# One inverse loop with other tiles beside it, a later down projection, and eight early ring tiles in a two-block kernel

## The chip, the cores and the metric

The kernel runs on one core of one Trainium2 chip. The metric is the device time of one execution in microseconds, the median of the runs shown. TensorE (PE), VectorE (DVE), ScalarE (ACT), GpSimd (POOL) and SyncE (SP) each work through a queue of their own in a fixed order. Transfers that SP or ACT issue run on 16 DMA engines.

## The reference, cut to what matters

Two blocks run one after the other on 512 tokens of width 1024. The first (RWKV, an MLP, an attention layer, another MLP) is the same before and after. The second is a mixer of two branches, and then 16 experts:

```python
proj = h @ w_in                      # qkv of DeltaNet, z, b, a, c_q, c_kv, k_r, gates
# DeltaNet, 8 heads of 128, forwards and backwards in time; per chunk:
lower = where(strict, (k_beta @ k.T) * decay, 0)
t_inv = inverse(eye + lower)         # unit triangular
u, w  = t_inv @ v_beta, t_inv @ (k_beta * exp(gc))
intra = where(tril, (q @ k.T) * decay, 0)
v_new = u - w @ state;  o = qd @ state + intra @ v_new   # then the state moves on
y_dn  = (rms_norm(o_fwd + o_bwd) * silu(z)) @ w_o_dn
y_mla = softmax_attention(c_q, c_kv, k_r) @ w_o_mla
x = x + gt1 * ((sigmoid(g_dn) * y_dn + sigmoid(g_mla) * y_mla) @ w_out)
# experts: each takes the 64 tokens that it scores highest
gate, idx = top_k(softmax(h @ w_router).T, 64)
hid = silu(xe @ w_gate) * (xe @ w_up)
out[idx] += (hid @ w_down) * gate
```

## The kernel before

A scheduler orders each engine's queue when the kernel is built, by a priority (the place in the program, plus an offset inside `behind`) and by its own idea of how long each instruction takes. On the chip the order is fixed: an instruction that has to wait holds up all that is behind it on its engine.

**The mixer** (`mixer`, from about 1620 us). `dn_group` runs the DeltaNet twice, for heads 0 to 3 and 4 to 7. Beside it, at lower priority, `mla_gen` feeds TensorE with dense tiles (`dense_gen`, the matmuls at L1323): 128 output columns each, 24 matmuls, and weights that SP loads, ACT rounds (L181) and POOL splits (L183). The order of the dense tiles is the list `cks`: 12 convolution tiles of the second group (`use_b`; `dn_conv` takes five DVE instructions for each), 8 z tiles (`use_z`, one ACT and one DVE instruction), 8 gate tiles (`use_g`, one ACT instruction), 7 latent tiles (`use_c`), 8 more gate tiles, then the projections of the MLA branch and its attention. The results go to DRAM through `keep`, a transfer that ACT issues (L1261), and come back through `fetch`, which SP issues.

One group goes through: the scaled keys and queries; four heads, each with its decay matrices E for both directions (L1545 to L1551, a strict mask on POOL) and the triangular matrices UB and masked products IN (L1556 to L1566; POOL adds the diagonal to E, L1564); the inverse `tri_inverse2`; and a scan over four chunks. UB holds 32 triangular matrices of 128x128, 16 upper ones (forwards) and 16 lower ones (backwards). The inverse first inverts the 32x32 blocks on the diagonals, one matrix to a partition: a DVE transpose into P (L1395), one loop of 31 steps that solves the one kind (L1400, L1402), a second loop of 31 steps for the other kind (L1407, L1409; on the other half each loop does nothing), and eight transposes back (L1413 into T1, L1414 into UB). Then products of 32-wide blocks (L1422, L1429) and of 64-wide ones (L1449, L1457, L1465) build the rest.

After both groups w_o_dn, w_o_mla and w_out follow (8 tiles each).

**The experts** (`experts`, from about 2498 us). They run in eight pairs. Weight tiles of 1 MiB (256 rows of one matrix of one expert) pass through a ring of RR = 16 slots of 8 KiB per partition; SP issues a slot's next load when TensorE has read it (L2081). A pair takes four steps of gate, four of up and four of down, each step two tiles and 16 matmul instructions (L2134, L2162), 24 tiles a pair, 192 in all. Between up and down stand: the one-hot matrix for the scatter and the gates (`slots`, L2095 to L2102), silu and product (L2146, L2147), and transposes (L2150, copied at L2152). RE = 5 of the slots lie where nothing is needed any more while w_out runs; SP issues their loads between the last w_out weight loads (`between`). The other 11 lie under the weight buffers, so that their first loads wait for the end of w_out. Gathers of the later pairs (`pieces`, L2068, L2069) are mixed into the steps of the first three pairs.

Of the kernel before, what the change touches and what calls it, by code (L numbers as in the profile page):

```python
# [34 lines left out]
RR = 16  # L35
RE = 5
RO = 1
SL = 38
# [84 lines left out]
class K:  # L123
# [1212 lines left out]
    def dn_gates(self, pt):  # L1336
# [46 lines left out]
        return dict(B=B, G=Gm, EG=EG, ET=ET, nEG=nEG, nB=nB, BL=BL)  # L1383

    def tri_inverse2(self, bp, UB):
# [30 lines left out]
        W1 = bp.tile([128, 32, 32], F32, name=self.nm("W1"), tag="p4", bufs=2)  # L1416

        xy = [(b + (d == 1), b + (d == 0), 16 * d) for b in (0, 2) for d in range(2)]
        pt = self.ps()
        for u in range(16):  # L1420
            for x, y, o in xy:
                nc.tensor.matmul(pt[Q[y], u * 32:u * 32 + 32], UB[Q[x], o + u, Q[y]], T1[Q[x], o + u],  # L1422
                                 start=(u == 0), stop=(u == 15), skip_group_check=True)
        nc.scalar.activation(W1[:, 0:16], pt.rearrange("p (u j) -> p u j", j=32), AF.Copy)
        yield 0.7
        pt = self.ps()
        for u in range(16):
            for x, y, o in xy:
                nc.tensor.matmul(pt[Q[x], u * 32:u * 32 + 32], W1[Q[y], u], UB[Q[y], o + u, Q[y]],  # L1429
                                 start=(u == 0), stop=(u == 15), skip_group_check=True)  # L1430
        for x, y, o in xy:
            p3 = pt[Q[x]].rearrange("p (u j) -> p u j", j=32)
            if x % 2:
# [5 lines left out]
        H = [slice(0, 64), slice(64, 128)]  # L1439
        xy = [(H[d], H[1 - d], 16 * d) for d in range(2)]  # L1440
        T2 = bp.tile([128, 16, 64], F32, name=self.nm("T2"), tag="p4", bufs=2)
        W2 = bp.tile([128, 16, 64], F32, name=self.nm("W2"), tag="p4", bufs=2)
        idn = self.cst("ident")
        pair = lambda pt: pt.rearrange("p (u j) -> p u j", j=64)
        for ub in (0, 8):
            pt = self.ps()
            for u in range(8):
                for x, y, o in xy:
                    nc.tensor.matmul(pt[x, u * 64:u * 64 + 64], UB[x, o + ub + u, x], idn[x, x],  # L1449
                                     start=(u == 0), stop=(u == 7), skip_group_check=True)  # L1450
            nc.scalar.activation(T2[:, ub:ub + 8], pair(pt), AF.Copy)
        yield 0.7
        for ub in (0, 8):
            pt = self.ps()
            for u in range(8):
                for x, y, o in xy:
                    nc.tensor.matmul(pt[y, u * 64:u * 64 + 64], UB[x, o + ub + u, y], T2[x, ub + u],  # L1457
                                     start=(u == 0), stop=(u == 7), skip_group_check=True)
            nc.vector.tensor_copy(W2[:, ub:ub + 8], pair(pt))
        yield 0.7  # L1460
        for ub in (0, 8):
            pt = self.ps()
            for u in range(8):
                for x, y, o in xy:
                    nc.tensor.matmul(pt[x, u * 64:u * 64 + 64], W2[y, ub + u], UB[y, o + ub + u, y],  # L1465
                                     start=(u == 0), stop=(u == 7), skip_group_check=True)
            for i, (x, y, o) in enumerate(xy):
                if i:
                    nc.vector.tensor_copy(UB[x, o + ub:o + ub + 8, y], pair(pt[x]))
                else:  # L1470
                    nc.scalar.activation(UB[x, o + ub:o + ub + 8, y], pair(pt[x]), AF.Copy)
# [19 lines left out]
    def dn_group(self, bp, tiles, gi, gs, Zs, out):  # L1491
# [41 lines left out]
        for i in range(4):  # L1533
# [900 lines left out]
```

## Time and profile before

| | |
|---|---|
| median of 3 runs | 2994.79 us (2993.59 to 2998.83) |
| the profiled execution | 2999.24 us, its span 2997.4 us |
| TensorE busy | 2766.3 us, 92% of the span |
| VectorE, ScalarE, GpSimd busy | 1615.5, 1049.1, 726.7 us |
| read from HBM | 471.26 MB |

Busy times say which engine a stage leans on; a stage's bound is read from what ends the idle time of its busiest engine. A DMA share near 1 means that all 16 DMA engines copy all the time. A wait is put down to what came last by the profile.

### The profile page before, as it was taken

What the parts mean: (1) busy time and instruction counts of PE and PEld (TensorE: products, weight loads), DVE (VectorE), ACT (ScalarE), POOL (GpSimd) and SP (SyncE); (2) the same over time, 40 slices, a digit from 0 to 9 for tenths busy, and PEclk for the clock granted to TensorE, in tenths of its full rate; (3) what the DMA queues carried; (4) which work ended last, traced back from release to release, by engine and by line L of the source; (5) the groups of instructions that cost most, each with busy time, mean ns of one, the idle gap of its engine ahead of it and who ended that gap; (6) DMA issues with size and microseconds to landing.
All of it is one profiled execution on the core that took longest, in us unless ns stands there. A gap on an engine that the chain in (4) does not pass through costs nothing. (4 is left out here: it accounts for less than half of the span.)

```text
span 2997.4 us, 38061 instructions
## 1 busy us (share of the span) xinstructions
PE 2766.3 (92%) x15046; PEld 1971.0 (66%) x15046; DVE 1615.5 (54%) x2449; ACT 1049.1 (35%) x1703; POOL 726.7 (24%) x563
## 2 busy tenths in 40 slices
PE   6998888999999999999999997998799997999997
PEld 1765666788876777788886775766677874444333
DVE  4568745465673367566636789638755442111112
ACT  2555523422234466422223542353344322110001
POOL 2456633211110043111113353144141121000000
PEclk9998777999999999999999999999999998999999
DMA  6324215355672321465432223142252359999998
GB/s 214 120 85 151 77 58 176 99 175 190 196 242 66 101 61 50 133 205 182 156 97 84 80 81 113 51 134 74 61 179 85 106 192 355 350 389 409 409 409 304
DMA packets 361010, 502.05 MB, mean 167 GB/s; under 512 B 24768, under 2 KB 236992, under 8 KB 360832
## 3 DMA queue, kind: packets, MB, share of 16 engines
q1 hardware_dynamic: 349600, 479.01, 47.0%
q10 hardware_dynamic: 11232, 20.62, 1.9%
q8 instruction: 118, 1.93, 0.3%
q14 instruction: 60, 0.49, 0.0%
HBM read 471.26 MB, written 26.21 MB: 166 GB/s over the span
## 5 line engine op out<-in xcount | busy, mean ns | idle before, releaser
L244 PE MATMUL psb<-s,wh 128*128 128x512 f32 x1384 | 542.8, 392 | 2.7 <-DVE s L988 1.9
L245 PE MATMUL psb<-s,wl 128*128 128x512 f32 x1384 | 540.4, 390 | 0.0
L246 PE MATMUL psb<-s,wh 128*128 128x512 f32 (+1 forms) x1320 | 514.7, 390 | 1.5 <-POOL s L481 0.6
L181 ACT ACTIVATE wh<-wr 128x1024 fp32r<-128x1024 f32 (+1 forms) x221 | 288.1, 1304 | 397.9 <-PE psb L246 263.9
L183 DVE TENSOR_TENSOR wl<-wr,wh 128x1024 fp32r<-128x1024 f32 (+1 forms) x145 | 260.7, 1799 | 262.8 <-ACT wh L181 260.4
L244 PEld LDWEIGHTS psb<-s,wh 128*128 128x128 f32 x1384 | 259.4, 187 | 70.7 <-issue 11.4
L245 PEld LDWEIGHTS psb<-s,wl 128*128 128x128 f32 x1384 | 259.5, 188 | 56.5 <-issue 2.2
L246 PEld LDWEIGHTS psb<-s,wh 128*128 128x128 f32 (+1 forms) x1320 | 247.4, 187 | 58.5 <-issue 2.9
L183 POOL TENSOR_TENSOR wl<-wr,wh 128x1024 fp32r<-128x1024 f32 (+1 forms) x76 | 185.5, 2443 | 401.4 <-ACT wh L181 386.1
L2134 PE MATMUL psb<-rg,s 128*64 128x512 f32 x1024 | 242.9, 597 | 5.7 <-DMA rg<-in_w_up_dram 4.4
L1323 PE MATMUL psf<-f,wh 128*128 128x512 f32 (+1 forms) x688 | 232.3, 412 | 10.7 <-ACT wh L181 10.7
L1019 POOL TENSOR_TENSOR s<-s 128x512 f32<-128x512 f32 x64 | 102.2, 1596 | 514.8 <-ACT s L1017 434.1
L2134 PEld LDWEIGHTS psb<-rg,s 128*64 128x64 f32 x1024 | 83.1, 136 | 142.6 <-issue 120.4
L1323 PEld LDWEIGHTS psf<-f,wh 128*128 128x128 f32 (+1 forms) x688 | 133.3, 195 | 42.5 <-ACT wh L181 11.6
L1323 PE MATMUL psf<-f,wl 128*128 128x512 f32 (+1 forms) x344 | 142.7, 415 | 16.6 <-POOL wl L183 16.5
L2162 PE MATMUL psb<-rg,s 128*64 128x512 f32 (+1 forms) x544 | 129.5, 620 | 0.0
L378 DVE SCALAR_TENSOR_TENSOR mt<-mr,crep,mt 128x512 f32<-128x512 f32 x168 | 126.4, 753 | 3.6
L201 ACT ACTIVATE s<-s 128x512 fp32r<-128x512 f32 x112 | 69.8, 625 | 136.2 <-POOL s L1019 73.1
L1026 DVE SCALAR_TENSOR_TENSOR s<-psb,aff,s 128x512 f32<-128x512 f32 x64 | 45.9, 751 | 129.1 <-PE psb L246 129.1
L1323 PE MATMUL psb<-f,wh 128*128 128x512 f32 (+1 forms) x336 | 106.5, 397 | 7.8 <-DVE f L479 5.9
L1017 ACT ACTIVATE s<-psb 128x512 f32<-128x512 f32 x64 | 37.6, 588 | 164.0 <-PE psb L246 164.0
L2162 PEld LDWEIGHTS psb<-rg,s 128*64 128x64 f32 x544 | 46.2, 147 | 73.9 <-issue 69.8
(565 smaller groups left out, 4926.4 us busy)
## 6 DMA issues: line engine op xcount, KB each, us to landing
rg<-in_w_gate_dram SPq DMA_DIRECT2D x64, 1024.0 KB
rg<-in_w_up_dram SPq DMA_DIRECT2D x64, 1024.0 KB
rg<-in_w_down_dram SPq DMA_DIRECT2D x64, 1024.0 KB
mr<-in_mod_w_dram SPq DMA_DIRECT2D x96, 512.0 KB
wr<-in_mlp_down_dram SPq DMA_DIRECT2D x32, 1024.0 KB
wr<-in_mlp_up_dram SPq DMA_DIRECT2D x31, 1024.0 KB
wr<-in_w_in_dram SPq DMA_DIRECT2D x54, 512.0 KB
mr<-in_w_mod_dram SPq DMA_DIRECT2D x40, 512.0 KB
```

Of the source, the lines that this page charges most:

```text
L181: nc.scalar.activation(hi, raw, AF.Copy)
L183: (lo_eng or self.lo_eng or nc.vector).tensor_tensor(lo, raw, hi.bitcast(F32), op=OP.subtract)
L201: nc.scalar.activation(hi, src, AF.Copy)
L244: nc.tensor.matmul(pt[:mw], hi[k][:, j:j + mw], a, start=(k == 0), stop=False)
L245: nc.tensor.matmul(pt[:mw], lo[k][:, j:j + mw], a, start=False, stop=False)
L246: nc.tensor.matmul(pt[:mw], hi[k][:, j:j + mw], b, start=False, stop=(k == nk - 1))
L378: nc.vector.scalar_tensor_tensor(acc[:, hb], raw[:, d], c, acc[:, hb], op0=OP.mult, op1=OP.add)
L1019: nc.gpsimd.tensor_tensor(sq, r, r, op=OP.mult)
L1026: nc.vector.scalar_tensor_tensor(xT[m], pt, gt[:, m:m + 1], xT[m], op0=OP.mult, op1=OP.add)
L1323: nc.tensor.matmul(pt[:rows, :cols], x, y, start=(k == 0 and q == 0), stop=(k == nk - 1 and q == 2))
L2134: nc.tensor.matmul(B[n][q], XE[hp][k0 // 2][:, o:o + 64], w[e][:, k, n * 512:n * 512 + 512], start=(k0 + k == 0), stop=(k0 + k == 7), skip ...
L2162: last = nc.tensor.matmul(pt[q, :n], HT[(k + i) // 4][:, o:o + 64], w[e][i], start=(k + i == 0), stop=(k + i == 7), skip_group_check=True)
```

## The change

- **Inverse.** The matrices of the backward direction are built transposed, so that all 32 are upper triangular and the second loop goes. Of the eight transposes back, two go (T1 is only needed for the blocks 0 and 2). The masked products IN of the backward direction need E the other way round: four TensorE transposes and an ACT copy for each head. POOL's addition of the diagonal goes (the mask now holds it). In the scan beta is now a row factor of the backward inverse: one DVE multiplication over half of UB per group, and one ACT copy in place of four scaled ones in each step of the backward direction. The products of 32-wide and 64-wide blocks change their places: they read two groups of rows instead of four, or one instead of two, and write different columns; per group 16 products that transpose 64-wide blocks, some copies, and a POOL copy and memset are added.
- **Order in a group.** `decays(i + 1)` is issued before `triangles(i)`.
- **Dense tiles beside it.** 8 convolution tiles, 8 gate tiles, the other 4 convolution tiles, 8 z tiles, 7 latent tiles, the other 8 gate tiles.
- **Experts.** The first gate step of the next pair is issued before a pair's transposes and down steps. `slots` multiplies the one-hot matrix by the scores, transposes it, and takes both the scatter matrix and the gates from there on DVE, without the eight small matmul instructions.
- **Ring.** RR 17, RE 8, slots SL 40; the early loads stand behind the 12th to 5th from last weight load (before: the 7th to 3rd from last).

```diff
-RR = 16
-RE = 5
-RO = 1
-SL = 38
+RR = 17
+RE = 8
+SL = 40
...
-        for k in range(31, 0, -1):
-            n, m = k, 32 - k
-            tv = tm[:, :n * m].rearrange("p (j i) -> p j i", i=m)
-            nc.vector.tensor_tensor(tv, P[:, 0:n, k:k + 1].to_broadcast([128, n, m]),
-                                    R[:, k:k + 1, k:32].to_broadcast([128, n, m]), op=OP.mult)
-            nc.vector.tensor_tensor(R[:, 0:n, k:32], R[:, 0:n, k:32], tv, op=OP.add)
-            yield 0.55
...
-        for d in range(4):
-            nc.vector.transpose(T1[Q[d]].rearrange("p u i -> p i u"), R[Q[d]].rearrange("p j i -> p i j"))
+        for d in (0, 2, 1, 3):
+            if d % 2 == 0:
+                nc.vector.transpose(T1[Q[d]].rearrange("p u i -> p i u"), R[Q[d]].rearrange("p j i -> p i j"))
             nc.vector.transpose(UB[Q[d], :, Q[d]].rearrange("p u j -> p j u"), R[Q[d]])
...
-        xy = [(b + (d == 1), b + (d == 0), 16 * d) for b in (0, 2) for d in range(2)]
+        xy = [(b, b + 1, b + 1 - d, 16 * d) for b in (0, 2) for d in range(2)]
...
+                nc.tensor.matmul(pt[y, u * 64:u * 64 + 64], UB[y, 16 + ub + u, y], idn[y, y],
+                                 start=(u == 0), stop=(u == 7), skip_group_check=True)
...
+        nc.gpsimd.tensor_copy(UB[x, 16:32, x], T2[1][x])
+        nc.gpsimd.memset(UB[x, 16:32, y], 0.0)
...
-                nc.gpsimd.tensor_tensor(v3(E), v3(E), bc(self.cst(strict)), op=OP.mult)
+                nc.gpsimd.tensor_tensor(v3(E), v3(E), bc(self.cst("le")), op=OP.mult)
...
+            pe = self.ps()
+            for cs in csl:
+                nc.tensor.transpose(pe[:, cs], Es[i][1][:, cs], idn)
...
-                nc.gpsimd.tensor_tensor(v3(E), v3(E), bc(idn), op=OP.add)
+                if d:
+                    E = self.s()
+                    nc.scalar.activation(E, pe, AF.Copy)
...
+        u1 = UB[:, 16:32].rearrange("p (i c) t -> p i c t", c=4)
+        nc.vector.tensor_tensor(u1, u1, gs["B"][:, :, 8 + 4 * gi:12 + 4 * gi].rearrange("p c i -> p i c").unsqueeze(3)
+                                .to_broadcast([128, 4, 4, 128]), op=OP.mult)
...
-        cks = self.fm_chunks(W, [[(m * 128, 128)] for m in self.dn_cols(1)], hf, use_b)
-        cks += self.fm_chunks(W, tl(3072, 8), hf, use_z)
-        cks += self.fm_chunks(W, tl(4960, 16), hf, use_g)
+        cv = self.fm_chunks(W, [[(m * 128, 128)] for m in self.dn_cols(1)], hf, use_b)
+        gc = self.fm_chunks(W, tl(4960, 16), hf, use_g)
+        cks = cv[:8] + gc[:8] + cv[8:] + self.fm_chunks(W, tl(3072, 8), hf, use_z) + gc[8:]
...
-        between = self.loads[-8:][RO:][:RE]
+        between = self.loads[-12:][:RE]
...
+            nc.vector.tensor_tensor(hv, hv, bc(aff), op=OP.mult)
...
+            nc.vector.tensor_scalar(OT[pr], pt, 0.0, None, op0=OP.is_gt)
+            nc.vector.tensor_reduce(gate[:, pr:pr + 1], pt, axis=AX.X, op=OP.add)
...
+        self.run(products(0))
+        for pr in range(8):
+            more = iter(())
+            if pr < 7:
+                more = products(pr + 1)
+                next(more)
...
                 for n in range(2):
                     add(Yp[n], range(4 * n, 4 * n + 4))
+                self.run(more)
```

`products(pr)` holds what stood in the loop of the pairs before: the steps of gate and up with the gathers between them, `slots`, silu and product. It gives way after each step, so that `next(more)` issues one gate step (two loads, 16 matmul instructions, a gather while there are any) and `self.run(more)` the other seven.

## Rows read from the trace of the kernel before

**Rows 1.** windows: length, then busy time (instructions) of each engine, clock, DMA share, GB/s

```profile
1760.00:1900.00 140.00, 112.57 (x774) 87.97 (x775) 126.95 (x204) 39.16 (x60) 50.59 (x24) 0.93 0.34 99
2040.00:2140.00 100.00, 71.19 (x575) 53.99 (x574) 92.48 (x151) 25.26 (x35) 29.65 (x13) 0.86 0.28 82
1740.00:2260.00 520.00, 446.88 (x3053) 356.24 (x3053) 370.59 (x663) 199.15 (x383) 187.64 (x103) 0.95 0.33 99
```

**Rows 2.** TensorE's waits, 1740 to 2260 us: total us, times, longest us

```profile
PE psb L1422 <- DVE T L1413: 27.2, 6, 13.2
PE psf L1323 <- POOL wl L183: 16.5, 11, 2.1
```

**Rows 3.** groups of instructions by line, 1600 to 2320 us: busy us, mean ns

```profile
L1407 DVE TENSOR_TENSOR tm<-P,R 128x31 f32<-128x31 f32 (+15 forms) x62 | 29.8, 480 | 2.0
L1409 DVE TENSOR_TENSOR R<-R,tm 128x31 f32<-128x31 f32 (+15 forms) x62 | 31.7, 511 | 2.1
L1413 DVE STREAM_TRANSPOSE T<-R 32x1024 f32<-32x1024 f32 x8 | 16.8, 2099 | 0.1
L1485 DVE SCALAR_TENSOR_TENSOR f<-psf,P,f 128x510 f32<-128x510 f32 (+1 forms) x48 | 35.6, 742 | 4.6 <-ACT f L1482 4.2
L1536 PE MATMUL psb<-C,s 128*128 128x128 f32 x32 | 4.9, 274 | 0.4 <-DVE in L1566 0.4
```

**Rows 4.** timelines by engine, one z tile beside the second loop: start us, us, instruction

```profile
1846.67 0.33 ACTq L1261 DMA_DIRECT2D kd<-f  x1
1847.04 0.60 ACT L1685 ACTIVATE f<-psf 128x512 f32<-128x512 f32 x1 [6.61 <-DVE tm L1407]
...
1848.67 2.51 POOL L183 TENSOR_TENSOR wl<-wr,wh 128x1024 fp32r<-128x1024 f32 x1 [5.77 <-ACT wh L181]
...
1849.00 2.44 DVE L1407 TENSOR_TENSOR tm<-P,R 128x231 f32<-128x231 f32 x1
1851.91 0.41 DVE L1407 TENSOR_TENSOR tm<-P,R 128x240 f32<-128x240 f32 x1
...
1851.24 0.50 PE L1323 MATMUL psf<-f,wl 128*128 128x512 f32 x1 [1.61 <-POOL wl L183]
```

**Rows 5.** TensorE's timeline: waits in the two groups, and 64-wide products of the inverse

```profile
1877.43 0.28 PE L1422 MATMUL psb<-T,UB 32*32 32x32 f32 x2 [10.26 <-DVE T L1413]
...
1897.60 2.08 PE L1449 MATMUL psb<-C,UB 64*64 64x64 f32 x60
...
2074.25 0.79 PE L1323 MATMUL psf<-f,wh 128*128 128x512 f32 x1 [10.69 <-ACT wh L181]
```

**Rows 6.** windows ahead of and in the experts' stage, columns as in group 1

```profile
2380.00:2420.00 40.00, 40.00 (x178) 32.88 (x177) 19.21 (x16) 11.28 (x13) 12.96 (x10) 1.00 0.33 99
2490.00:2690.00 200.00, 185.00 (x914) 86.61 (x916) 28.86 (x57) 30.49 (x53) 1.23 (x1) 0.94 0.92 359
2690.00:2960.00 270.00, 255.44 (x1092) 108.14 (x1088) 44.71 (x75) 20.12 (x34) 0.00 (x0) 0.98 1.03 408
```

**Rows 7.** timeline, the turn from up to down: the first pair, then the second

```profile
2532.45 3.65 PE L2134 MATMUL psb<-rg,s 128*64 128x512 f32 x16
...
2540.02 0.66 PE L2150 MATMUL psb<-C,s 128*128 128x128 f32 x4 [2.52 <-DVE s L2147]
2542.57 1.11 PE L2150 MATMUL psb<-C,s 128*128 128x128 f32 x4 [1.90 <-DVE s L2147]
2543.62 6.02 PE L2162 MATMUL psb<-rg,s 128*64 128x512 f32 x16
...
2606.83 0.66 PE L2095 MATMUL psb<-C,s 128*128 128x128 f32 x4
...
2613.10 3.68 PE L2162 MATMUL psb<-rg,s 128*64 128x512 f32 x8
```

**Rows 8.** SP's timeline: loads into the ring

```profile
2470.43 11.77 SPq L2081 DMA_DIRECT2D rg<-in_w_up_dram  x8
2501.42 6.58 SPq L2081 DMA_DIRECT2D rg<-in_w_down_dram  x4
```

More of the change, by code (lines that the diff above doesn't have):

```diff
@@ L1427, in tri_inverse2 @@
         for u in range(16):
[L1428 to L1429 removed]
+            for x, y, z, o in xy:
+                nc.tensor.matmul(pt[Q[z], u * 32:u * 32 + 32], T1[Q[y], o + u], UB[Q[y], o + u, Q[y]],
                                  start=(u == 0), stop=(u == 15), skip_group_check=True)
[L1431 to L1433 removed]
+        for x, y, z, o in xy:
+            p3 = pt[Q[z]].rearrange("p (u j) -> p u j", j=32)
+            if o:
                 nc.scalar.activation(UB[Q[x], o:o + 16, Q[y]], p3, AF.Copy)
@@ L1437, in tri_inverse2 @@
         yield 1.2
[L1439 to L1442, printed above, removed]
+        x, y = slice(0, 64), slice(64, 128)
+        T2 = [bp.tile([128, 16, 64], F32, name=self.nm("T2"), tag="p4", bufs=2) for _ in range(2)]
         idn = self.cst("ident")
@@ L1447, in tri_inverse2 @@
             for u in range(8):
-                for x, y, o in xy:
-                    nc.tensor.matmul(pt[x, u * 64:u * 64 + 64], UB[x, o + ub + u, x], idn[x, x],
+                for d, q in enumerate((x, y)):
+                    nc.tensor.matmul(pt[q, u * 64:u * 64 + 64], UB[x, 16 * d + ub + u, x], idn[x, x],
                                      start=(u == 0), stop=(u == 7), skip_group_check=True)
-            nc.scalar.activation(T2[:, ub:ub + 8], pair(pt), AF.Copy)
+            nc.vector.tensor_copy(T2[0][x, ub:ub + 8], pair(pt[x]))
+            nc.scalar.activation(T2[1][x, ub:ub + 8], pair(pt[y]), AF.Copy)
         yield 0.7
@@ L1455, in tri_inverse2 @@
             for u in range(8):
-                for x, y, o in xy:
-                    nc.tensor.matmul(pt[y, u * 64:u * 64 + 64], UB[x, o + ub + u, y], T2[x, ub + u],
+                for d, q in enumerate((y, x)):
+                    nc.tensor.matmul(pt[q, u * 64:u * 64 + 64], UB[x, 16 * d + ub + u, y], T2[d][x, ub + u],
                                      start=(u == 0), stop=(u == 7), skip_group_check=True)
-            nc.vector.tensor_copy(W2[:, ub:ub + 8], pair(pt))
+            nc.scalar.activation(T2[0][y, ub:ub + 8], pair(pt[y]), AF.Copy)
+            nc.vector.tensor_copy(T2[1][y, ub:ub + 8], pair(pt[x]))
         yield 0.7
+        pts = []
         for ub in (0, 8):
@@ L1463, in tri_inverse2 @@
             for u in range(8):
[L1464 to L1471, printed above, removed]
+                v = T2[0][y, ub + u], UB[y, ub + u, y]
+                nc.tensor.matmul(pt[x, u * 64:u * 64 + 64], *v, start=(u == 0), stop=(u == 7), skip_group_check=True)
+                v = UB[y, 16 + ub + u, y], T2[1][y, ub + u]
+                nc.tensor.matmul(pt[y, u * 64:u * 64 + 64], *v, start=(u == 0), stop=(u == 7), skip_group_check=True)
+            nc.vector.tensor_copy(UB[x, ub:ub + 8, y], pair(pt[x]))
+            nc.scalar.activation(UB[y, 16 + ub:24 + ub, x], pair(pt[y]), AF.Copy)
+            pt = self.ps()
+            for u in range(8):
+                nc.tensor.matmul(pt[y, u * 64:u * 64 + 64], UB[y, 16 + ub + u, y], idn[y, y],
+                                 start=(u == 0), stop=(u == 7), skip_group_check=True)
+            pts.append(pt)
+        for ub, pt in zip((0, 8), pts):
+            nc.scalar.activation(UB[y, 16 + ub:24 + ub, y], pair(pt[y]), AF.Copy)
+        nc.gpsimd.tensor_copy(UB[x, 16:32, x], T2[1][x])
+        nc.gpsimd.memset(UB[x, 16:32, y], 0.0)
         yield 1.0
@@ L1532, in dn_group, with decays @@
         csl = [slice(c * 128, c * 128 + 128) for c in range(4)]
-        for i in range(4):
+        def decays(i):
             pv = self.ps()
@@ L2121, in experts, with products @@
             gather(0, f)
-        for pr in range(8):
+        SG = [None] * 8
+        def products(pr):
             hp = pr // 2
-            G = [self.ps() for _ in range(2)]
-            U = [self.ps() for _ in range(2)]
+            G, U = [], []
             for W, B in ((A["w_gate_2"], G), (A["w_up_2"], U)):
+                B.extend(self.ps() for _ in range(2))
                 for k0 in range(0, 8, 2):
@@ L2147, in experts @@
                 nc.vector.tensor_tensor(sg, U[n], sg, op=OP.mult)
+                SG[pr].append(sg)
+        self.run(products(0))
[4 more added lines that the diff above has]
+                next(more)
+            HT = []
+            for sg in SG[pr]:
                 pt = self.ps()
```

60 lines of the change are left out of this document (34 added, 26 removed).

## The prediction

> **What bounds the kernel now.** I read three views in this order: the windows by stage, then for each stage where TensorE isn't full its waits, then the timelines of the engines named there. The change touches two stretches: the mixer (about 1620 to 2470 us) and the experts (about 2500 us to the end).
>
> In the mixer TensorE carries the time: dense tiles of low priority fill what DeltaNet leaves, and outside the two groups it is full. From 1740 to 2260 us it works 446.9 of 520 us, so 73.1 us are idle [rows 1]. In the two stretches around the inverses (1760 to 1900, 2040 to 2140 us) VectorE is busy 91% and 92% of the time, and TensorE is idle 27.4 and 28.8 us, 56 us together: there VectorE is the bound. The granted clock is 0.93 and 0.86 there, which means that TensorE ran part of these stretches at the lower of its two levels (1.2 GHz instead of 2.4). The waits name the causes: 27.2 us for the transposes L1413 that end the loops, 16.5 us for POOL's split of a dense weight [rows 2], and one of 10.69 us for ACT's rounding of one [rows 5]. The second cause is VectorE again: in the timelines ACT's queue stands at the store of a z tile (issued at 1846.67) until VectorE, deep in the loop, has made the tile; only then do ACT's next steps and POOL's split (1848.67) follow, and TensorE has waited 1.61 us at 1851.24 [rows 4].
>
> In the experts' stage two limits take turns. From 2690 to 2960 us the DMA share is 1.03 at 408 GB/s: the engines copy all the time [rows 6]. A 1 MiB tile takes 1.049 MB / 408 GB/s = 2.57 us. From 2490 to 2690 us the share is only 0.92: the ring is full and TensorE frees it too slowly. Lost copying: (1.03 - 0.92) / 1.03 x 200 = 21 us. As copying sets the end, only these 21 us, and what is copied ahead, can be won.
>
> **Experts: the later down projection.** At a turn TensorE ends the up step at 2532.45 + 3.65 = 2536.1 us, waits 2.52 and 1.90 us for silu and product, and ends the first down step at 2543.62 + 6.02 = 2549.6 us (6.02 instead of 3.65, its clock being low after the gaps) [rows 7]. That is 13.5 us for a step of 3.65, 9.9 us lost. In the second pair the turn runs from 2606.83 to 2613.10, and 8 instructions take 3.68 us instead of 1.83: 6.3 + 1.85 = 8.1 us lost. Afterwards a gate step of the next pair (3.65 us of work that is only moved) covers VectorE's part. This part grows: the scatter matrix and the gate sum come ahead of the products, some four steps of 0.7 us (the 0.742 us of a 512-wide step [rows 3] as the nearest price), 2.8 us, which just fits under 3.65. What remains is three times four transposes (0.66 each) and a copy (0.60), 2.6 us. Saved: 7.3 and 5.5 us; in the third pair the copying has nearly caught up, I take 1. On SP two gate loads go ahead of eight down loads; the ring takes tiles in the order in which they are read, so nothing waits longer for that.
>
> **Experts: the ring.** SP issues the tiles that wait for the end of w_out from 2470.43 us on, and the next only at 2501.42, when TensorE has freed a slot [rows 8]. Between these 16 tiles are in the ring before and 17 after, however many came early: one tile, 2.6 us. The three further early loads thus buy no 3 x 2.57 = 7.7 us but only the room for the 17th slot, since the DMA engines would be idle sooner. Their place on SP is between weight loads that TensorE needs; what is queued behind them is the next w_o_mla or w_out load. From 2380 to 2420 us, where some of them now fall, the share is 0.33 with TensorE full [rows 6], so I cost them at 0 (bounds 0 and 7.7). The Trainium skill, "DMA: Bandwidth & Descriptors", section "Issuing engines are not separate DMA queues", says that all transfers share the same 16 engines and interleave; by that alone the full 7.7 us would be charged and the sum below be 29 in place of 37; the share of 0.33 speaks for the smaller charge.
>
> Experts together: 7.3 + 5.5 + 1 + 2.6 = 16 us won. Bounds: 3 (only the ring) and 21 (all that was lost).
>
> **Mixer: the inverse.** The second loop costs VectorE 29.8 + 31.7 = 61.5 us in both groups, and four of the eight L1413 transposes 8.4 us [rows 3]. This is time of VectorE; what counts is TensorE's wait. (a) The 27.2 us arise because TensorE's queue holds the first L1422 products ahead of dense tiles that could run, and the loops end later than the scheduler thought. With half of the loops I take half: 13.6 us won (bounds 0 and 27.2). What is late next is the first loop, which stays. (b) Gate tiles have no VectorE step, so ACT's queue no longer stands at their store: the three waits beside the z tiles (1.61 us and two alike, 5.3 us) go. Four convolution tiles, each with four VectorE steps of 0.742 us and one more, leave the loop for the scan; I take 4 us of the other waits for POOL. Together 9 us (bounds 0 and 16.5). (c) The 10.69 us stand beside latent tiles, which still meet the second inverse; I take 3 (bounds 0 and 10.7). (d) With half of the long gaps some of the time at the lower clock goes; 3 us (bounds 0 and 10, from 0.07 x 140 = 9.8 us in the first stretch).
>
> Added: 32 transposes of E, at 4.9 us for 32 alike [rows 3]; 32 instructions of 64-wide transposes per group, at 2.08 us for 60 [rows 5], 2.2 us in both. Sum 7 us of TensorE, charged in full. The products of small blocks now read the same rows in pairs. If such pairs ran one after the other, five stages of about 2 us would double, 20 us in both groups; the nearest row says otherwise: half-width experts' products that share rows take 3.65 / 16 = 0.23 us for 512 columns, where a full-width product takes 4.9 / 32 = 0.15 for 128. So 0, bound 20. VectorE's new multiplication (4 x 0.742 = 3.0 us) and POOL's copy (near the 2.5 us of a split [rows 4]) lie between inverse and scan, on DeltaNet's own chain; dense tiles cover them on TensorE. Without that cover they cost 11 us. ACT's eight copies (0.60 each) replace more scaled copies than they are, and POOL loses sixteen additions. The eight gate tiles pass four convolution tiles on SP, ACT, POOL and TensorE, each with load, split, 24 products and store; the fetches of the second group wait for these four. They come right behind the gate tiles, so I expect them done within the scan: 0.
>
> One rule speaks against (b). In the timelines a loop instruction of 0.41 us takes 2.44 while POOL's split runs [rows 4]. The Trainium skill, "SBUF — State Buffer", section "SBUF: two separate sides", has VectorE and GpSimd share a port pair that whoever starts first holds for the whole instruction. Dense tiles that no longer stall bring more splits into a loop, each 2 us; with two or three more per group, half of it felt by TensorE, the mixer would give 16 instead of 21 us.
>
> Mixer together: 13.6 + 9 + 3 + 3 - 7 = 21 us won.
>
> **The sum.** 16 + 21 = 37 us. The profiled execution would go from 2999.2 to 2962 us (its span from 2997.4 to 2960); the median, 4.4 us lower, from 2994.8 to 2958.
>
> **Rivals.**
> 1. TensorE fills nearly all: the waits of 27.2, 16.5 and 10.7 and a few others go (60 us), less 7 added. For it: VectorE's load in the two stretches falls by about a third. Against: the order on TensorE is still made ahead of time. 53 + 21 = 74 won: 2921 us.
> 2. The mixer's waits only move: the L1422 wait and the splits stall elsewhere for as long, and the experts give 16: 2979 us. For it: a VectorE loop is still there, and z and latent tiles now meet the second inverse.
> 3. The turn isn't shortened, since VectorE's longer part comes after the gate step: only the ring's 2.6 us in the experts, 24 in all: 2971 us.
> 4. Slower: the tiles that need VectorE (8 z, 7 latent), shifted back by the gate tiles, meet the second group's loop. Each z tile stalls ACT's queue and with it TensorE by 2 us (17 us); the two normalisations of latent tiles each make a wait like that of 10.69 us with a low clock behind it (30 us instead of the 15 so far); the L1422 waits stay, and 7 us are added, while the 5 us beside the z tiles go: 17 + 15 + 7 - 5 = 34 us, of which the experts give back 16: 3013 us. It decides from the point where new waits in the mixer exceed the gains by 16 us. Against it: VectorE loses 70 us of work in these stretches.
>
> **How the numbers follow.** Forecast 0.50, rival 1 0.20, rival 2 0.13, rival 3 0.10, rival 4 0.07. Predicted: 2958 us; its own range is 2940 to 2972. The range 2918 to 2984 leaves out rival 4, and of rivals 1 and 2 the outer third. About 0.2% (6 us) is what a measurement of this kernel can tell from no change. Slower: rival 4, 0.07. Within 0.2%: 0.05, the end of rival 2. Faster: 0.88.
>
> **What would show it.** The second loop's lines gone and VectorE's load between the groups lower; TensorE's wait at the first 32-wide products at about 14 us instead of 27; no 1.6 to 2 us waits beside the gate tiles; the start of the experts some 20 us earlier; the DMA share from the first experts' product on near 1.03 after some 20 us, and no gap of over 1 us ahead of the down steps. It is wrong if the experts start as late as before, if the share stays near 0.92 for 200 us, or if a new wait of over 10 us stands in the second group.

## The result and the profile after

The changed kernel takes 2976.45 us (median of 7 executions), the kernel before, beside it, 2994.79: ratio 0.9942, 95% interval 0.9914 to 0.997. That is 18 us, just under half of the 37 that were forecast. The kernel is faster, as said, and clear of noise; the time lies outside the forecast's own range (2940 to 2972) and inside the wider one (2918 to 2984). One thing was not in the forecast at all: before, all executions lie within 5.5 us; after, they lie between 2962 and 2992 us, and their mean granted clock falls nearly in the order of the times, from 0.961 at 2962 us to 0.950 at 2992. As an estimate from these numbers, for a TensorE that is busy all the time, (0.961 - 0.950) x 2976 = 33 us: the clock alone is of the size of the spread. The profiled execution is the one of the median, 2976.45 us with a span of 2974.6.

Windows of the changed kernel (columns as in [rows 1]):

```profile
1740.00:2260.00 520.00, 465.86 (x3178) 375.75 (x3177) 310.12 (x551) 212.03 (x380) 166.87 (x90) 0.93 0.33 100
2380.00:2420.00 40.00, 39.13 (x173) 32.07 (x172) 20.01 (x15) 11.19 (x14) 17.27 (x13) 1.00 0.84 288
2490.00:2540.00 50.00, 50.00 (x259) 23.38 (x258) 3.29 (x6) 9.56 (x16) 0.00 (x0) 0.98 0.88 342
2540.00:2690.00 150.00, 149.53 (x714) 67.42 (x714) 32.01 (x52) 20.52 (x36) 0.00 (x0) 1.00 1.02 404
2690.00:2960.00 270.00, 254.55 (x1065) 101.90 (x1063) 54.54 (x82) 22.74 (x36) 0.00 (x0) 1.00 1.00 393
```

The experts look as forecast: from 2540 us on the DMA share is 1.02 and TensorE's clock is 1.00; over the whole of 2490 to 2690 us the share is 0.98, where [rows 6] had 0.92. The early ring tiles now fill 2380 to 2420 us (share 0.84, before 0.33), with TensorE still busy 39.13 of 40 us. In the mixer VectorE is busy 310 us instead of 371 and TensorE 466 of 520 us instead of 447. So 19 us of idle time are gone there, but the clock column has fallen from 0.95 [rows 1] to 0.93: as an estimate from these two, TensorE was at the lower level for some 73 us of the stretch instead of 52, and part of the 19 us is the same work taking longer. The experts begin only 7 us earlier, where some 20 were forecast; the first instruction of their gather, before and after:

```profile
2494.42 0.55 PE L2068 MATMUL psb<-s,s 128*128 128x256 f32 x1 [0.94 <-DVE s L2058]
```

```profile
2487.30 0.55 PE L2100 MATMUL psb<-s,s 128*128 128x256 f32 x1 [0.94 <-DVE s L2090]
```

So of the 22.8 us between the two spans some 16 are won in the experts and 7 ahead of them. TensorE's waits in the mixer's stretch:

```profile
PE psb L1415 <- DVE T L1407: 22.7, 2, 11.8
PE psf L1322 <- DVE f L1811: 10.8, 1, 10.8
PE psb L1688 <- DVE s L1690: 4.0, 1, 4.0
PE psb L1427 <- DVE T L1422: 3.9, 2, 2.6
PE psf L1322 <- POOL wl L182: 3.8, 3, 2.2
PE psb L1688 <- POOL s L1682: 3.7, 2, 2.7
PE psf L1322 <- DVE f L1491: 2.8, 2, 2.1
```

The wait ahead of the first small products (L1415, before L1422) is 22.7 us; [rows 2] had 27.2 and I wanted 13.6. POOL's splits cost 3.8 instead of 16.5. The wait of 10.69 us for ACT's rounding is gone, and one of 10.8 us for VectorE's rope step (L1811) stands 110 us later. The waits at L1688, 7.7 us, answer to 5.6 us at L1657 before.

The row that I take to lie behind the 30 us between executions is a small one: the 3.9 us at L1427, the second set of small products. Here is TensorE at the end of the first loop of either group (some rows of the timeline; a number in brackets is the idle time ahead):

```profile
1822.53 0.32 PE L1415 MATMUL psb<-T,UB 32*32 32x32 f32 x4 [10.91 <-DVE T L1407]
1832.90 0.31 PE L1427 MATMUL psb<-UB,T 32*32 32x32 f32 x2 [2.62 <-DVE T L1422]
1844.39 3.67 PE L1445 MATMUL psb<-C,UB 64*64 64x64 f32 x60
...
2075.82 0.32 PE L1415 MATMUL psb<-T,UB 32*32 32x32 f32 x4 [11.81 <-DVE T L1407]
2086.22 0.24 PE L1427 MATMUL psb<-UB,T 32*32 32x32 f32 x2 [1.33 <-DVE T L1422]
2092.51 2.07 PE L1445 MATMUL psb<-C,UB 64*64 64x64 f32 x60
```

The same 60 records take 3.67 us in the first group and 2.07 in the second (2.08 in [rows 5]). The windows say why: between the two sets the clock was 1.00, and then it is 0.50 for 30.7 us, with TensorE busy all the time. In the second group it is 0.51 around the long wait and 1.00 afterwards:

```profile
1826.50:1832.80 6.30, 3.78 (x135) 2.75 (x133) 6.24 (x4) 1.54 (x2) 2.01 (x1) 1.00 0.01 3
1832.80:1863.50 30.70, 30.60 (x382) 24.76 (x383) 6.22 (x10) 8.42 (x14) 5.79 (x6) 0.50 0.18 53
2068.00:2082.00 14.00, 6.18 (x118) 4.72 (x122) 13.87 (x18) 6.44 (x9) 4.96 (x3) 0.51 0.19 56
2082.00:2104.00 22.00, 20.67 (x429) 16.08 (x418) 10.98 (x13) 8.69 (x15) 6.69 (x4) 1.00 0.25 74
```

30.6 us of work at half the clock would take at best 15.3 at full, so such a stretch costs up to 15 us. Theory: the small products run at 1.2 GHz in none, one or both of the groups, and that took the missing gain. Rivals: it lies in the new waits or the added products, the same in every execution; or in the experts.

### The profile page after: what moved, and what is told of

It is laid out like the page before. It is cut to its first block, busy times and chain, and to the rows that moved or that the text cites. A ratio compares the mean times of both kernels' runs of the same rounds, so it can differ in the third digit from the quotient of the medians.

```text
span 2974.6 us, 38010 instructions
## 1 busy us (share of the span) xinstructions
PE 2771.8 (93%) x15078; PEld 1976.9 (66%) x15078; DVE 1560.9 (52%) x2339; ACT 1057.5 (36%) x1692; POOL 708.1 (24%) x551
## 4 chain that ended last, share of the span: by engine, by line
PE 73%; DVE 13%; DMA 7%; issue 3%; ACT 3%; POOL 1%; SPq 1%; ACTq 0%; DVEq 0%; POOLq 0%
PE psb L243 11%; PE psb L245 11%; PE psb L244 11%; PE psb L2166 6%; PE psf L1322 5%; PE psb L1322 3%; PE psb L2206 3%; DMA rg<-in_w_down_dram 2%; DMA rg<-in_w_up_dram 1%; PE psb L1223 1%; DVE R L1401 1%; DVE s L1491 1%; PE psm L341 1%; PE psm L1957 1%; DVE tm L1399 1%
## 5 line engine op out<-in xcount | busy, mean ns | idle before, releaser
L243 PEld LDWEIGHTS psb<-s,wh 128*128 128x128 f32 x1384 | 259.6, 188 | 71.0 <-issue 11.4
L2166 PE MATMUL psb<-rg,s 128*64 128x512 f32 x1024 | 254.8, 599 | 6.3 <-DMA rg<-in_w_up_dram 5.7
L2214 DVE SCALAR_TENSOR_TENSOR s<-psb,gate,s 128x512 fp32r<-128x512 f32 (+1 forms) x17 | 12.1, 719 | 164.3 <-ACT s L2213 163.9
```

Source lines behind the costliest of these rows:

```text
L243: nc.tensor.matmul(pt[:mw], hi[k][:, j:j + mw], a, start=(k == 0), stop=False)
L2166: nc.tensor.matmul(B[n][q], XE[hp][k0 // 2][:, o:o + 64], w[e][:, k, n * 512:n * 512 + 512], start=(k0 + k == 0), stop=(k0 + k == 7), skip ...
```

## The experiments

**The two halves of the change alone.** The first kernel is before with the experts' part:

```diff
-RR = 16            +RR = 17
-RE = 5             +RE = 8
-for pr in range(8):   # gate, up, silu, down in turn
+self.run(products(0)) ...  next(more); ... down of pr ...; self.run(more)
```

> The kernel before with the experts' part of the change alone (down projection later, slots, 17 ring tiles with 8 early); the mixer is as before. Theory: the experts' term of the forecast is right, 16 us, and the spread of the changed kernel's times (30 us, against 5.5 before) comes from the mixer: about 2979 us, spread under 8 us. Rival: the experts are what varies (their product waits or the copying): spread over 20 us, and a gain that differs by execution.

Measured: 2980.28 us against 2996.05, ratio 0.9947 (0.9935 to 0.9959), 15.8 us; executions within 8.1 us. In its trace the share from 2540 to 2690 us is 1.02. The experts' 16 us are real, and they don't carry the spread.

The second is before with the mixer's part (one loop, transposed blocks, order of decays and triangles, gate tiles beside):

> The kernel before with the mixer's part alone (one loop, transposed blocks, order of decays and triangles, gate tiles beside the loop); the experts are as before. Theory: the mixer's term was mis-sized because TensorE, after the wait for the loop's end, runs the small products at 1.2 GHz for a time that varies by execution: median 2985 to 2992, spread over 15 us, fastest executions near 2975 (the 20 us of the forecast). Rival, the added products and new waits (10.8 us at the rope, 4.0 and 2.7 at the end of a group): the same 7 us in every execution, 2988, spread under 8 us.

Measured: 2993.45 us, ratio 0.9982 (0.9965 to 0.9999), 12 executions in three clusters: three at 2976 to 2978 us, seven at 2989 to 2995, two at 3004. The fastest have the mean clock 0.957, the slowest 0.949. The profiled one, at 2993.56, has the long stretch in the *other* group. Windows over the 64-wide products of both groups:

```profile
1839.50:1849.90 10.40, 10.40 (x231) 9.08 (x230) 4.79 (x7) 5.85 (x10) 4.09 (x3) 1.00 0.01 3
2082.30:2102.00 19.70, 19.70 (x233) 16.35 (x232) 4.26 (x7) 5.58 (x10) 4.34 (x3) 0.50 0.15 42
```

The same 231 to 233 instructions take 10.4 or 19.7 us. I read the clusters as no, one and both groups in the long stretch: then the mixer's part gives 2996 - 2977 = 19 us where none falls into it, nearly the 21 of the forecast, and each group that does costs 11 to 16. Only the middle cluster has a trace, so the other two are inferred, from the mean clocks. The rival of a fixed loss falls: no fixed wait makes three clusters.

**The ring alone.** Before, with 17 ring tiles, 8 of them early, and the down projection in its old place:

```diff
-RR = 16  -RE = 5  -SL = 38        +RR = 17  +RE = 8  +SL = 40
-between = self.loads[-8:][RO:][:RE]
+between = self.loads[-12:][:RE]
```

> The kernel before with the ring alone (17 tiles, 8 of them early, 40 slots); the down projection comes as before. By the forecast one tile more is in the ring: 2.6 us, 2993 where the kernel before shows 2996. If the three further early tiles count in full: 7.7 us, 2988. If early tiles hold up the weights that TensorE needs: 2996 or more. The rest of the 16 us that the experts' part gave (2980) is then the later down projection.

Measured: 2994.29 against 2996.43 us, ratio 0.9988 (0.9979 to 0.9997): 2.1 us, interval 0.9 to 6.3. The forecast's 2.6 is within, a full 7.7 is not. What remains of the 15.8 us, some 13, is the later down projection.

**The old order of the dense tiles.** The changed kernel, with z tiles beside the loop and gate tiles last:

```diff
-cks = cv[:8] + gc[:8] + cv[8:] + self.fm_chunks(W, tl(3072, 8), hf, use_z) + gc[8:]
+cks = cv + self.fm_chunks(W, tl(3072, 8), hf, use_z) + gc
```

> The changed kernel with the dense tiles in the old order (convolution, z, gate), so z tiles stand beside the first inverse again. If the gate tiles beside the loop are worth the 9 us that the forecast gave them: 2985. If the order of the tiles is worth nothing, because the same waits come elsewhere (rope tiles beside the second group): 2976. If the low clock of the first group hangs on which dense tiles stand beside the small products, the spread falls under 10 us, whatever the median.

Measured: 2982.05 us (2968 to 2989), ratio 0.9944 (0.9924 to 0.9965). The spread stays, so the gate tiles are not what brings the low clock. Their worth can't be read from the medians; the fastest executions, at like mean clock (0.960 and 0.961), differ by 6 us (2968 and 2962), less than the 9 I had charged; this compares two single executions.

**What lowers the clock: the long wait?** Two kernels are built on the changed one, with useless 448-wide products of constants on TensorE. In the first they fill the wait ahead of L1415:

```diff
+for _ in range(22):
+    nc.tensor.matmul(pf[:, 0:448], self.C[:, 0:128], self.C[:, 0:448], ...)
 for u in range(16):          # first small products
```

> The changed kernel with 22 useless 448-wide products of constants on TensorE ahead of each group's first small products, where it waited 10.9 and 11.8 us for the loop's end; a like product, 512 wide, takes 0.592 us alone and nearer 0.5 in a row, so they fill some 11 us. Nothing real is moved. Theory A (the idle wait drops the clock, and the small products then hold it low): the granted clock is 1.0 through the products of both groups, no stretch of 27 to 31 us at 1.2 GHz, times in one cluster at 2962 to 2966, some 12 us under the changed kernel's median. Theory B (the small products alone let the clock fall, whatever came before): the same long stretches after the products begin, times spread over 2962 to 2992 as those of the changed kernel. Theory C (the clock isn't what varies): 2976, same spread.

Measured: 2988.96 us (2977 to 3000). My price of the useless products was wrong: the 22 of the first group ran from 1813.0 to 1829.7 us, 0.76 us each and not 0.5, so 16.7 us lay in waits of 10.9 and 11.8, and the whole is later by some 11. But the reading stands, in a trace of the slowest of the twelve executions (3000.22 us):

```profile
1800.00:1830.00 30.00, 28.89 (x142) 18.05 (x142) 28.60 (x45) 4.63 (x6) 7.59 (x3) 1.00 0.35 105
2055.00:2090.00 35.00, 32.92 (x235) 20.61 (x233) 33.72 (x52) 9.77 (x13) 9.80 (x5) 1.00 0.20 53
1843.10:1862.60 19.50, 19.50 (x233) 16.64 (x232) 4.80 (x7) 5.40 (x9) 5.44 (x5) 0.50 0.14 42
2100.80:2119.00 18.20, 18.20 (x231) 15.97 (x230) 4.25 (x7) 4.04 (x8) 1.97 (x2) 0.50 0.11 30
```

The long waits are gone and the clock full ahead of the products, and still both groups run their 64-wide products at 0.50. Theory A falls. What is left in both groups is a wait ahead of the *second* set, 2.2 and 4.0 us.

**Or the small products themselves?** In the second kernel the useless products stand among the 64-wide ones:

```diff
 for u in range(8):
+    if u % 4 == 0:
+        nc.tensor.matmul(pf[:, 0:448], self.C[:, 0:128], self.C[:, 0:448], ...)
     ...                      # 64-wide products
```

> The changed kernel with two useless 448-wide products of constants among each 16 of the 64-wide products (16 to a group, some 7.5 us to a group at the full clock, 15 us in all); the wait ahead of them stays. Theory B (the small products let the clock fall and stay low): with wide products among them it comes back or never falls, no long stretch; times in one cluster at 2962 + 15 = 2977, spread under 8 us. Theory A or C: long stretches as before, 2977 to 3007.

Measured: 3019.33 us (3018 to 3024). Each useless product took 0.95 us among the others at full clock, so they lengthen a group's 64-wide part by some 12 us (23.1 against 11.4 in the changed kernel's second group), 24 and not 15 in both. Two of the 16 of a group ran earlier than meant, among the second set of small products. The windows of the 64-wide products:

```profile
1840.50:1863.60 23.10, 23.10 (x254) 12.96 (x254) 4.79 (x7) 5.00 (x10) 3.08 (x4) 1.00 0.01 1
2098.90:2140.80 41.90, 41.90 (x254) 22.06 (x253) 4.22 (x7) 4.73 (x8) 1.97 (x2) 0.50 0.00 1
```

One group is at full clock from end to end, the other at half from end to end, with the same 254 instructions and the same wide products among them. So theory B falls in this form too: in the second group wide work among the small products didn't bring the clock back. In both groups the level at which the 64-wide products begin is kept until they are done. The five executions stand within 6 us, as theory B also had it, but with a long stretch in the one that was traced.

**Theory D** was formed from these traces: what decides is whether TensorE waits *inside* the chain of small products, ahead of the second set. The traces of all kernels, two groups each (the wait is the idle time ahead of the second set, the clock that of the 64-wide products):

| wait ahead of the second set | groups | clock 1.00 | clock 0.50 |
|---|---|---|---|
| under 1 us (before, experts alone, ring alone, both loops with later products, and every group with enough dense work ahead of the second set) | 16 | 15 | 1, falling in the midst, behind a wait of 1.6 us |
| 1.3 to 4.0 us (the changed kernel and those with its order there) | 12 | 3, two of them with a short fall ahead of the 64-wide products | 9 |

The direct trial is the changed kernel with its first products where they were, so that both long waits stay, and only the second set and the first 64-wide products put behind some more dense matmuls in TensorE's queue:

```diff
+mm = nc.tensor.matmul(pt[:rows, :cols], x, y, ...); self.dm.append(mm.ins)   # dense tiles
+with self.tc.issue_after(self.dm[(357, 910)[gi]]):
     ...                      # second set of small products
+with self.tc.issue_after(self.dm[(373, 924)[gi]]):
     ...                      # first 64-wide products
```

> The changed kernel, its first small products where they were (the waits of 10.9 and 11.8 us stay), only the second set and the 64-wide products issued behind some more dense matmuls (36 and 32 between first and second set, 16 and 14 more ahead of the 64-wide ones), so that TensorE doesn't wait ahead of them. Theory D: no stretch over 14 us at 1.2 GHz in either group, the executions in one cluster at the fast end of the changed kernel's, 2960 to 2966. Rival A, the long waits ahead of the first products lower the clock: spread 2962 to 2992 as in the changed kernel. Rival B, the small products themselves: the same.

Measured: 2958.6 us (2957.5 to 2963.8), ratio 0.9876 (0.9862 to 0.989). Its waits ahead of the first products, in the first and in the second group:

```profile
PE psb L1416 <- DVE T L1408: 10.9, 1, 10.9
PE psb L1416 <- DVE T L1408: 11.8, 1, 11.8
```

And the windows of the first long wait and of both groups' 64-wide products:

```profile
1811.00:1822.00 11.00, 0.11 (x4) 0.09 (x4) 10.28 (x23) 0.00 (x0) 1.80 (x1) 0.70 0.18 48
1839.40:1848.80 9.40, 9.40 (x229) 8.50 (x228) 4.10 (x6) 3.45 (x6) 4.38 (x4) 1.00 0.22 59
2078.80:2088.20 9.40, 9.40 (x229) 8.47 (x228) 4.10 (x6) 3.45 (x6) 1.97 (x2) 1.00 0.23 59
```

Both long waits are untouched, 10.9 and 11.8 us, the clock even falls around them, and yet the executions stand together within 6.2 us, 18 us under the changed kernel's median. This is theory D's forecast (2960 to 2966), a little exceeded. So theory A falls here too.

Theory D is not the whole of it, though. In the second group of this kernel no wait of over 0.5 us is left in the chain, and still the clock fell behind the second set. It came back under the dense matmuls of the second anchor, just before the 64-wide products began at 2078.84 us. The kernel with the mixer's part alone has a like row in its first group, ahead of the 64-wide products that ran at 1.00. First this kernel's row, then that one's:

```profile
2074.70:2078.10 3.40, 3.40 (x10) 2.63 (x9) 0.69 (x1) 2.27 (x4) 2.11 (x1) 0.50 0.21 77
```

```profile
1832.50:1835.90 3.40, 3.40 (x10) 2.30 (x10) 0.70 (x1) 0.93 (x2) 0.16 (x1) 0.50 0.72 211
```

A fall alone thus does not cost the chain; the clock can be back before the 64-wide products. This leaves a rival that no run separates: every edit that filled a wait also put dense matmuls right ahead of a link, and it may be these, and not the missing wait, that keep the clock up or bring it back. The edit has two anchors; which of them does more was not tried apart.

**Covering the long waits too.** Four kernels, each with anchors at or behind those of the one before it, or more of them. The first only puts the first products 48 and 53 dense matmuls later (`self.dm[(369, 930)[gi]]`):

> The changed kernel, with the first small products of both groups issued 48 and 53 dense matmuls later on TensorE, so that dense work lies where TensorE waited 10.9 and 11.8 us for the loop's end. Theory (the wait, and the low clock that follows it, took the mixer's gain): the 22.7 us of waits go to a few us, the 30.7 us stretch at 1.2 GHz becomes shorter, 25 to 35 us faster than the changed kernel: 2942 to 2952, spread under 15 us. Rival, the waits only move (dense tiles wait for their split weights instead, or DeltaNet's chain sets the end and is only put back): 2970 to 2980. Between: the waits go and the clock stays low, 2955.

Measured: 2968.63 us (2966 to 2974), ratio 0.9914 (0.9901 to 0.9927): 25 to 35 us were expected against the changed kernel, 8 came. The waits fell from 22.7 to 7.7 us, but in the first group a wait of 2.5 us ahead of the second set was left, and the clock was low for 44 us.

The second: first products at `(414, 930)`, second set at `(428, 942)`.

> As the kernel with the first small products 48 and 53 dense matmuls later, but in the first group 93 later (another 8 us of waits stood there), and the second set of products 12 to 14 dense matmuls behind the first. Theory: the waits of 4.4, 3.3 and 2.5 us in the first group go: 8 to 10 us faster than that kernel, 2959; and if the clock then holds, 44 us at 1.2 GHz shorter as well, 2948. Rival, dense tiles run out of split weights, which VectorE's loop and ACT's queue hold up: 2966 to 2970, the wait at the dense tiles instead.

Measured: 2954.83 us (2953 to 2960), ratio 0.9862 (0.9849 to 0.9874). That is 14 us under the kernel ahead of it, where 8 to 10 were expected from the waits alone and 21 with the clock held. A wait of 3.7 us was left ahead of the second set of the first group, and its products were at 0.50 again.

The third: second set at `(448, 942)`, first 64-wide products at `(464, 952)`.

> As the kernel with the first small products 93 and 53 dense matmuls later, and now dense matmuls also fill what is left ahead of the second set in the first group (34 between the sets instead of 14; a wait of 3.7 us stood there) and ahead of the 64-wide products (16 and 10). Theory D, from the traces so far: the clock falls at the second set of small products if TensorE has waited ahead of it, and the level at which the 64-wide products begin is kept to their end (low to the end in 9 groups, full to the end in 5). So no long stretch in either group: 34 us at half clock in the first group go (some 13 us) with 3.7 us of wait: 2938 to 2944, spread under 8 us. Rival B, small products lower the clock by themselves: long stretches stay in some executions, 2951 to 2960.

Measured: 2950.79 us (2946 to 2954), ratio 0.9844 (0.9829 to 0.9859), 7 us slower than the slow end of theory D's forecast and next to the fast end of rival B's (2951 to 2960). Its trace shows what was left. TensorE now waited 1.6 us ahead of the second 64-wide products of the first group, and 2.6 us behind it the clock fell and stayed low to their end. The wait, and then the windows around it:

```profile
PE psb L1458 <- ACT f L1497: 1.6, 1, 1.6
```

```profile
1853.00:1855.40 2.40, 0.88 (x3) 0.39 (x3) 2.33 (x5) 0.89 (x3) 2.04 (x1) 1.00 0.00 0
1855.40:1858.00 2.60, 2.55 (x60) 2.15 (x62) 1.10 (x2) 1.61 (x4) 1.34 (x2) 0.99 0.44 45
1858.00:1871.60 13.60, 13.60 (x127) 12.07 (x122) 5.63 (x6) 2.85 (x6) 2.05 (x3) 0.50 0.16 52
```

So a fourth anchor, at the second 64-wide products (`self.dm[(478, 964)[gi]]`):

> As the kernel with dense matmuls ahead of the first, the second and the first 64-wide products (2950.8 us), and 14 and 12 more ahead of the second 64-wide products. There TensorE still waited 1.6 us in the first group, and the clock fell behind it, from 1858 to 1871.6. Theory D (a wait inside the chain of small products lowers the clock until they end): the wait and the low stretch go, 1.6 us and half of 13.6: 2942 to 2945. If the fall at 1858 had another cause: 2949 to 2951, the stretch at 1.2 GHz still there.

Measured: 2937.9 us (2935 to 2941), ratio 0.9806 (0.9793 to 0.982): 58 us faster than before, 39 faster than the change, and the fastest version here. Theory D had 2942 to 2945; where the 4 us beyond that come from is open. No wait of over 0.9 us is left inside the chain of either group, and both run their 64-wide products at full clock:

```profile
1853.20:1866.10 12.90, 12.77 (x242) 11.00 (x241) 9.63 (x15) 8.20 (x13) 7.00 (x5) 1.00 0.39 113
2067.10:2078.50 11.40, 11.40 (x239) 10.15 (x238) 4.40 (x7) 5.58 (x9) 4.28 (x3) 1.00 0.33 100
```

**Is the one loop needed for that?** The last kernel asks what the anchors do with both loops: before, with the experts' part, first products at `(565, 1098)`, second set at `(577, 1110)`.

> What the one loop is worth by itself: the kernel before with the experts' part (2980 us), both loops and the old order, but the first small products 83 and 96 dense matmuls later, the second 12 behind them, so that TensorE's waits of 9.9 and 13.0 us ahead of the first products are covered here too. If the waits, and not VectorE's work, are what the mixer's time hangs on: 2980 less 23 to 27 us, 2953 to 2957, nearly as fast as the changed kernel with its waits covered (2951). If VectorE's second loop sets the end through DeltaNet's own chain: dense tiles run out later, 2965 to 2980.

Measured: 2990.65 us (2988 to 2996), ratio 0.999 (0.9981 to 0.9999), 10 us *slower* than without the anchors and outside both forecasts. In the second group the dense tiles that should have covered the loops are those of the queries, and they need VectorE themselves, whose rope step stands behind the loop in its queue:

```profile
PE psf L1322 <- DVE f L1783: 36.4, 1, 36.4
```

With two loops, in the old order of the tiles and with these anchors, the dense work free of VectorE did not reach to cover them; with one loop and the new order it did. That the one loop is needed for this is not shown: the order of the tiles differs too, and another place for the anchors with two loops was not tried.

## Why the prediction was wrong in the mixer and right in the experts

- **Experts, 16 us: right.** 15.8 alone. The waits ahead of the transposes of silu's product, of which [rows 7] had the first, and the same waits of the changed kernel with those that follow them in its list, from the first experts' product to the end:

```profile
PE psb L2150 <- DVE s L2147: 20.1, 11, 2.5
```

```profile
PE psb L2206 <- DMA rg<-in_w_down_dram: 7.2, 11, 1.2
PE psb L2166 <- DMA rg<-in_w_up_dram: 5.7, 9, 0.7
...
PE psb L2194 <- DVE s L2181: 0.8, 4, 0.2
```

  20.1 us have become 0.8, so VectorE's longer part fits under the gate step; what TensorE waits for now is the ring. Ring and turn divide as forecast, 2.6 and 13.8 against 2.1 and some 13. Rival 3 is out.
- **Mixer, 21 us: the step that failed first is (d)**, the low clock; alone the mixer's part gave 2.6 us in the median. I booked 3 us of *gain*, from the rule that fewer long gaps give less time at 1.2 GHz. The bounds were 0 and 10, with no loss among them, though I had seen a low clock behind gaps in the experts [rows 7]; and the 10 came from the first stretch alone, where the second, at 0.86 over 100 us, holds another 14. In truth the time at the lower level grew, by some 20 us in the profiled execution (the estimate of 73 against 52), which at half speed is a loss of some 10 us in place of the gain of 3. The long waits ahead of the chain did not decide the clock of the 64-wide products; the low clock came with waits of 1.3 to 4 us between two sets of small products, and the change makes such waits. With two loops the first set was issued in pieces beside dense tiles, and the second followed without a wait of over 0.8 us; the waits inside the chain of the kernel before:

```profile
PE psb L1465 <- DVE W L1459: 1.6, 1, 1.6
PE psb L1429 <- issue: 0.8, 1, 0.8
PE psb L1429 <- ACT W L1424: 0.7, 1, 0.7
```

  With one loop the first set comes at once, and its copies (L1422) stand on VectorE behind three transposes:

```profile
1826.24 5.89 DVE L1408 STREAM_TRANSPOSE UB<-R 32x1024 f32<-32x1024 f32 x3
1832.16 0.68 DVE L1422 COPY T<-psb 32x512 f32<-32x512 f32 x1
```

  Nothing in my list of added waits named this one: I had charged the products and copies and not what is queued ahead of the copies. With the gaps filled and both long waits left, the time is 2958.6 us, the 2958 of the forecast; some of that agreement is chance, as the next points show.
- **(a), half of the 27.2 us: wrong too, 22.7 stayed, 9 us short of the forecast.** I halved the wait because half of the loops go. But the wait is not a share of the loop: as I read it, it is the time by which the loop ends later than TensorE's queue was laid out for, and the queue was laid out anew. In the first group TensorE reaches L1415 at 1811.6 and the loop ends at 1820.35. In that loop six instructions take 1.84 to 2.50 us instead of 0.2 to 0.4, and each of them stands beside one of POOL's six splits, as here:

```profile
1804.14 2.64 POOL L182 TENSOR_TENSOR wl<-wr,wh 128x1024 fp32r<-128x1024 f32 x1 [0.36 <-ACT wh L180]
1804.57 2.50 DVE L1401 TENSOR_TENSOR R<-R,tm 128x256 f32<-128x256 f32 x1
```

  Together that is some 11 us, the size of the wait. In the second group it does not add up so: three instructions of the loop take 2.49 to 2.52 us, some 6 us lost, and the wait is 11.8. The pattern is that of [rows 4] and of the Trainium skill, "SBUF — State Buffer", section "SBUF: two separate sides", that VectorE and GpSimd share a port pair. No run here took the splits off POOL, so that they are the wait's cause is argued for the first group, and for some half of the wait in the second.
- **(b) and (c), 9 and 3 us.** POOL's waits fell by 12.7 us, more than forecast, and the 10.69 us went. But the rope wait of 10.8 us came, and 2.1 us more at the end of a group. The sum is near the forecast, its parts are not.
- **Row-sharing products, 0 with bound 20: right in the stage compared.** At full clock the 60 records take 2.07 us where [rows 5] had 2.08.
- **Rival 2** (waits only move) comes nearest to the median, but for another reason: at full clock the gain is there. Something like rival 4's mechanism, dense tiles that need VectorE behind its loop, shows in the kernel with both loops and anchors (36.4 us, there with the tiles of the queries).

What stays open: why a like wait lowers the clock to the end of the chain in nine groups and not in three (2.5 and 2.7 us among these), and so why the same kernel takes 2962 us in one execution and 2992 in another. Nor is it the wait alone: the clock also fell behind the second set where TensorE had waited under 0.5 us, and before, TensorE waited 1.6 us in the second group ahead of the last 64-wide products, which there read other rows in pairs, and the clock stayed at 1.00. Whether the row-sharing products bear on that was not tried.

## What to carry to other kernels

A median hides a choice between two levels: when the executions of a changed kernel spread wider than those before, look for a stretch whose clock differs from trace to trace, and read the same instructions in both. Around a chain of small products the short waits inside the chain were worth filling first (18 us here), by putting independent wide matmuls ahead of each link in TensorE's queue, then the long one ahead of it; the fill must not need the engine that one waits for. Halving the work behind a wait doesn't halve the wait when the order of the queues is made anew; look for the difference between where the waiting engine arrives and where the work ends.

## What the runs showed of the hardware

- A granted clock of 0.50 lasted over a chain of small products though TensorE was busy all the time (30.60 of 30.70 us), and even with products of 448 columns among them (41.9 us at 0.50). In the nine groups of the table it came back only with the work behind the chain; where it had fallen ahead of the 64-wide products (the two rows of 3.40 us above), it was back among dense matmuls before they began. The Trainium skill, "TensorE: Matmul & The Clock Gate", section "Part 1: The HAM clock gate (the "warmup" mystery)", has the clock released by activity; an engine that is busy in the trace's sense did not get it back here, so busy time alone is not what to go by.
- An idle time of 11 us ahead of the chain, with a clock of 0.70 over it, did not lower the 64-wide products' clock: they ran at 1.00 in the kernel whose chain had no wait of over 0.5 us.
- A product of unsplit 32-bit operands, 448 wide, stands in the trace as two records and takes 0.76 us in a row (33.4 us for the 44 of both groups) and 0.95 among small ones, while 16 of the experts' 512-wide ones take 3.65 us [rows 7], 0.23 each:

```profile
L1417 PE MATMUL psb<-C 128*128 128x448 f32 x88 | 33.4, 539 | 0.0
```
